# Inverting the delta-rule blocks of a prompt from 16-row pieces on 128 lanes instead of 32-row pieces on 64

## The chip, the cores and the metric

The kernel runs on one core of one Trainium2 chip. Its time is the device time of one execution in microseconds (us); a profiled execution gives besides it the span from the first to the last instruction, in which all traces below are read. TensorE is called PE in the profile, VectorE DVE, ScalarE ACT, GpSimdE POOL and SyncE SP; PEld is PE's loading of weights. Each has its own instruction queue and works through it in order.

## The reference, cut to what matters

The program is one decoder layer with two token mixers (sparse attention and gated DeltaNet) for a prompt of 256 tokens and a decode step of 8 sequences. The change lies in DeltaNet's prompt half, for 8 heads of width 128. In the reference's chunk step:

```python
L = jnp.exp(jnp.where(tril, dec[..., :, None] - dec[..., None, :], -jnp.inf))
kb = kc * bc[..., None]
A = jnp.where(stril, jnp.einsum('bhik,bhjk->bhij', kb, kc) * L, 0.0)
Tm = lax.linalg.triangular_solve(eye + A, jnp.broadcast_to(eye, A.shape),
                                 left_side=True, lower=True, unit_diagonal=True)
u = Tm @ vb
w = Tm @ (kb * jnp.exp(dec)[..., None])
```

What must be computed is the inverse of a unit lower-triangular matrix, for each head and chunk; `u` and `w`, the recurrence over chunks, the gate `z` and two projections follow from it. The kernel uses chunks of 128 tokens, so there are 2 chunks x 8 heads = 16 matrices of 128x128.

## The kernel before

**The stream of weights.** Nearly all of the work is a list `halves` of weight blocks of 128x1024 values. Each is loaded by SP (`raw`), split by ACT into a rounded part `hi` (L332) and by DVE into the rest `lo` (L333), and PE adds three products per 128x128 piece into the PSUM tile `acc`: a half is 24 matmuls with 264 columns (`three`, L316). `raw`, `hi` and `lo` have three buffers each, `acc` two. DVE also merges finished projections (`gate`, L1489; `zt`, L1468).

**Generators beside the stream.** Everything else (attention, decode, DeltaNet) is written as Python generators that are resumed by `tick()` twice per half; `yield n` lets n ticks pass. This order of writing, and then a scheduler with modelled durations, sets the order of the instructions on PE, DVE and ACT at build time. The order on SP and POOL is the order of writing. So a weight matmul may stand before, between or behind the matmuls of a generator, and on the chip each queue keeps the order that was fixed then.

**The inverse**, in `g_gdn`, L1187 to L1260. `At` (128 rows, 2 chunks, 8 heads, 128 columns) holds A. Diagonal blocks of 32 rows, 4 per matrix, 64 in all, are copied by four POOL DMAs to a DRAM tile `ad` (L1190), and from there into `lanes`, one block on each of 64 partitions (L1196). DVE inverts them row by row, i = 1 to 31, with one product of i*i values (L1203) and one sum over them (L1204) per row; both read and write 64 partitions. The result and its transpose go to the DRAM tile `td` (L1210, L1211) and back as diagonal blocks into `U` (L1215, 4 DMAs) and `TI` (L1218, 2 DMAs); `U` holds transposed inverses, `TI` plain ones. Two merge levels on PE double the blocks, 32 to 64 and 64 to 128. Each level goes over four quads (chunk t, four heads hg): a first matmul of A with U into a PSUM tile `inv`, a copy to SBUF by ACT (`P1`; at the last level also the transposed block, `T1`), a second matmul with the plain inverse, and a negated copy into U by DVE (L1239, L1259). `PG("inv")` takes turns in two PSUM banks. Then `uw` (L1270) multiplies U with the values and keys of each head, and `dS`, `og`, `vn` carry the recurrence.

**Slots.** Large tiles (`lanes`, `prod`, `U`, the decode states `sst`, ...) share 13 SBUF slots. A tile waits for the last reader of the one that had its slot. `TI` is the end of `prod`.

**Decode beside it.** `g_gdn_dec` runs at the same time: for each pair of sequences `sw` (16 matmuls), `swt` (4 transposes), `vnb` (16 transposes), with ACT and DVE updating the state `sst` (L1437, L1438), which is then written out as `o_Ss`.

## Time and profile before

| what | value |
|---|---|
| time, median of 3 runs | 1154.9 us (1154.56 to 1155.14) |
| profiled execution, its own time | 1156.45 us |
| its span | 1154.8 us |
| PE busy | 1116.2 us (97%) |
| DVE busy | 724.4 us (63%) |
| ACT busy | 570.6 us (49%) |
| POOL busy | 140.0 us (12%) |
| mean granted clock of PE | 0.981 |

The page says for each engine how long it was busy, then slices of the span, then the chain of work that ended last. A line of a group has the source line, engine, operation, `out<-in` by tile names, and shapes. A matmul of float32 data stands as two records in the trace, a weight matmul of the stream as one. In answers by windows, the numbers behind a stretch are its length, the busy time of PE, PEld, DVE, ACT and POOL with the number of instructions in brackets, the granted PE clock (1.00 is full), the DMA engines' share and GB/s.

### The profile page before, as it was taken

How to read it: one execution, taken by the hardware profiler on the slowest of the kernel's cores; microseconds unless marked ns; L12 is line 12 of the kernel's file. 1: busy time of each engine (PE TensorE's matmuls, PEld its weight loads, DVE VectorE, ACT ScalarE, POOL GpSimd, SP SyncE). 2: the span in 40 equal slices, each digit the busy share in tenths (PEclk: the TensorE clock that was granted, in tenths of full speed). 3: DMA queues.
4: the chain of work that ended last, by engine and by line, in shares of the span. 5: the costliest groups of instructions: out<-in, count | busy, mean ns of one | idle time of the engine just before them, and what ended most of it. 6: DMA issues, size and time to landing. Idle time of an engine off the chain costs nothing.

```text
span 1154.8 us, 24861 instructions
## 1 busy us (share of the span) xinstructions
PE 1116.2 (97%) x9334; PEld 1072.1 (93%) x9334; DVE 724.4 (63%) x1538; ACT 570.6 (49%) x1126; POOL 140.0 (12%) x217
## 2 busy tenths in 40 slices
PE   3999999999999999999999999999978999999998
PEld 3989999999999987897889999999967999999998
DVE  3487665444667766873565585679954565477543
ACT  4455655444634766773455465453421464444332
POOL 4420344100001320112113000000010000000000
PEclk9999999999999999999999999999985999999999
DMA  8874577335436874589979554664660345556663
GB/s 296 258 231 140 192 216 204 122 114 164 164 128 198 221 194 139 158 223 226 343 289 394 178 179 164 204 221 153 231 178 1 107 156 181 183 182 218 202 239 128
DMA packets 76843, 222.86 MB, mean 193 GB/s; under 512 B 10465, under 2 KB 27370, under 8 KB 75186
## 3 DMA queue, kind: packets, MB, share of 16 engines
q1 hardware_dynamic: 59346, 164.36, 43.3%
q0 software_dynamic: 14784, 45.70, 13.8%
q10 hardware_dynamic: 2592, 11.21, 2.6%
q8 instruction: 73, 1.20, 0.4%
q14 instruction: 48, 0.39, 0.1%
HBM read 203.23 MB, written 17.99 MB: 192 GB/s over the span
## 4 chain that ended last, share of the span: by engine, by line
PE 85%; DVE 6%; DMA 1%; issue 1%; ACT 0%; POOL 0%; POOLq 0%; ACTq 0%; DVEq 0%
PE acc L205 70%; DVE lanes L1204 2%; PE inv L205 1%; DVE lo L333 1%; PE po L205 1%; PE gtr L202 1%; PE pvo L205 1%; PE ps L205 1%; PE gsc L205 1%; PE cf L205 1%; DVE prod L1203 1%; PE kk L205 1%; PE vnb L202 1%; DMA U<-td 1%; DVE sst L1438 1%
## 5 line engine op out<-in xcount | busy, mean ns | idle before, releaser
L205 PE MATMUL acc<-xh,hi 128*128 128x264 f32 (+1 forms) x1488 | 433.5, 291 | 0.0
L332 ACT ACTIVATE hi<-raw 128x1024 fp32r<-128x1024 f32 (+1 forms) x250 | 264.0, 1057 | 334.6 <-PE acc L205 263.2
L205 PE MATMUL acc<-xh,lo 128*128 128x264 f32 (+1 forms) x1488 | 426.7, 287 | 2.2 <-DVE lo L333 2.2
L205 PE MATMUL acc<-xl,hi 128*128 128x264 f32 (+1 forms) x1488 | 427.4, 287 | 0.0
L333 DVE TENSOR_TENSOR lo<-raw,hi 128x1024 fp32r<-128x1024 f32 (+1 forms) x250 | 304.2, 1218 | 194.2 <-ACT hi L332 191.9
L205 PEld LDWEIGHTS acc<-xh,hi 128*128 128x128 f32 (+1 forms) x1488 | 281.3, 189 | 7.4 <-issue 7.0
L205 PEld LDWEIGHTS acc<-xh,lo 128*128 128x128 f32 (+1 forms) x1488 | 280.5, 188 | 4.6 <-DVE lo L333 2.6
L205 PEld LDWEIGHTS acc<-xl,hi 128*128 128x128 f32 (+1 forms) x1488 | 281.6, 189 | 1.4 <-issue 1.0
L205 PE MATMUL acc<-hi,w1h 128*128 128x254 f32 (+1 forms) x512 | 147.7, 289 | 16.5 <-ACT hi L409 16.5
L205 PE MATMUL acc<-lo,w1h 128*128 128x254 f32 (+1 forms) x512 | 146.4, 286 | 3.9 <-DVE lo L410 3.6
L205 PE MATMUL acc<-hi,w1l 128*128 128x254 f32 (+1 forms) x512 | 144.9, 283 | 0.0
L410 DVE TENSOR_TENSOR lo<-rawc,hi 128x512 fp32r<-128x512 f32 (+2 forms) x136 | 83.9, 657 | 51.4 <-ACT hi L409 46.2
L205 PEld LDWEIGHTS acc<-hi,w1h 128*128 128x128 f32 x512 | 97.8, 191 | 16.9 <-ACT hi L409 16.7
L409 ACT ACTIVATE hi<-rawc 128x512 fp32r<-128x512 f32 (+2 forms) x136 | 74.6, 599 | 58.8 <-PE acc L205 54.6
L205 PEld LDWEIGHTS acc<-lo,w1h 128*128 128x128 f32 x512 | 98.5, 192 | 5.2 <-DVE lo L410 5.0
L205 PEld LDWEIGHTS acc<-hi,w1l 128*128 128x128 f32 x512 | 98.2, 192 | 0.1
L386 POOL DMA_DIRECT2D rawc<-ccmp x125 | 67.6, 541 | 100.1 <-issue 71.2
L205 PE MATMUL acc<-oh,hi 128*128 128x264 f32 x256 | 73.3, 286 | 1.5 <-DVE gate L1489 1.4
L205 PE MATMUL acc<-mh,hi 128*128 128x264 f32 x256 | 72.6, 284 | 0.0
L205 PE MATMUL acc<-ol,hi 128*128 128x264 f32 x256 | 72.5, 283 | 0.0
L205 PE MATMUL acc<-ml,hi 128*128 128x264 f32 x256 | 72.5, 283 | 0.0
L205 PE MATMUL acc<-oh,lo 128*128 128x264 f32 x256 | 72.5, 283 | 0.0
(450 smaller groups left out, 1508.7 us busy)
## 6 DMA issues: line engine op xcount, KB each, us to landing
raw<-win SPq DMA_DIRECT2D x184, 512.0 KB, 3.5
raw<-wpab SPq DMA_DIRECT2D x32, 512.0 KB, 3.4
raw<-wo SPq DMA_DIRECT2D x32, 512.0 KB, 3.8
rawc<-ccmp SPq DMA_DIRECT2D x126, 128.0 KB, 3.1
rawc<-ccmp POOLq DMA_DIRECT2D x125, 128.0 KB, 3.2
raw<-w SPq DMA_DIRECT2D x8, 512.0 KB, 5.3
wk<-winK SPq DMA_DIRECT2D x8, 512.0 KB, 7.7
o_wk<-wk POOLq DMA_DIRECT2D x8, 512.0 KB, 8.6
```

The source lines that it names most:

```text
L202: T.transpose(out, in_, ident[0:n, 0:n])
L205: T.matmul(out, lhsT, rhs, start=start, stop=stop, **k)
L332: S.activation(self.hi, self.raw, AF.Copy)
L333: V.tensor_sub(self.lo, self.raw, self.hi)
L386: e.dma_start(rawc[kv, b][j // 8][:, j % 8].rearrange("p s c g -> p (s c g)"), src[kv, bass.ds(r, 1)].rearrange("o d f -> (o d) f"))
L409: S.activation(h, src, AF.Copy)
L410: V.tensor_sub(l, src, h)
L1203: V.tensor_tensor(pp, Lt[:, 0:i, 0:i], La[:, i, 0:i, None].to_broadcast([64, i, i]), ALU.mult)
L1204: V.tensor_reduce(Lt[:, i, 0:i], pp.rearrange("p j c -> p c j"), AX.X, ALU.add, negate=True)
L1438: V.scalar_tensor_tensor(ss[:, b, h, :], p4[:, 128 * hh:128 * hh + 128], k[:, c:c + 1], ss[:, b, h, :], ALU.mult, ALU.add)
```

## The change

Blocks of 16 rows instead of 32: 8 per matrix, 128 in all, one on each of the 128 partitions. Rows i = 1 to 15 instead of 1 to 31. `La` and `Lt` become part of `prod` (`lanes` is no longer a slot), `U` takes its slot before `prod` does, and U and TI are zeroed by DVE before the rows instead of U alone behind them. `ad` is filled by 8 DMAs instead of 4, U by 8 instead of 4, TI by 4 instead of 2. A merge level from 16 to 32 is added; at the level from 32 to 64 the plain inverse is made by multiplying U with the identity and copied to TI by ACT, since td no longer holds it. All three levels are written as `first`, `second`, `third` per quad, with the second matmul of one quad behind the first matmul of the next. The generator yields about as many ticks as before in all. Diff, with the last helper whole:

```diff
@@ -1184,80 +1184,102 @@
             yield 4
         del L["qkv", 1], kTg
 
-        ad = dp.tile([4, 16, 32, 32], F32, name="ad")
-        td = dp.tile([2, 4, 16, 32, 32], F32, name="td")
-        for k in range(4):
+        ad = dp.tile([8, 16, 16, 16], F32, name="ad")
+        td = dp.tile([2, 8, 16, 16, 16], F32, name="td")
+        for k in range(8):
             G.dma_start(ad[k].rearrange("h i j -> i h j"),
-                         At[32 * k:32 * k + 32, :, :, 32 * k:32 * k + 32].rearrange("i t h j -> i (t h) j"))
-        lanes = slot("lanes", [64, 2, 32, 32])
+                        At[16 * k:16 * k + 16, :, :, 16 * k:16 * k + 16].rearrange("i t h j -> i (t h) j"))
+        U = slot("U", [128, 2, 8, 128])
         prod = slot("prod", [128, 1536])
         TI = prod[:, 1024:1536].rearrange("p (h j) -> p h j", j=32)
+        lanes = prod[:, 256:768].rearrange("p (a i j) -> p a i j", a=2, i=16)
         La, Lt = lanes[:, 0], lanes[:, 1]
         G.dma_start(La.rearrange("p i j -> p (i j)"), ad.rearrange("k h i j -> (k h) (i j)"))
         V.memset(Lt, 0.0)
-        V.memset(lanes[:, 1].rearrange("p i j -> p (i j)")[:, ::33], 1.0)
+        V.memset(Lt.rearrange("p i j -> p (i j)")[:, ::17], 1.0)
+        V.memset(U, 0.0)
+        V.memset(TI, 0.0)
         yield 6
-        cost = 0
-        for i in range(1, 32):
-            pp = prod[0:64, 0:i * i].rearrange("p (j c) -> p j c", c=i)
-            V.tensor_tensor(pp, Lt[:, 0:i, 0:i], La[:, i, 0:i, None].to_broadcast([64, i, i]), ALU.mult)
+        for i in range(1, 16):
+            pp = prod[:, 0:i * i].rearrange("p (j c) -> p j c", c=i)
+            V.tensor_tensor(pp, Lt[:, 0:i, 0:i], La[:, i, 0:i, None].to_broadcast([128, i, i]), ALU.mult)
             V.tensor_reduce(Lt[:, i, 0:i], pp.rearrange("p j c -> p c j"), AX.X, ALU.add, negate=True)
-            cost += 0.4 + 2 * i * i / 960.0
-            if cost > 2.2:
-                cost = 0
-                yield 2
+            if i % 3 == 2:
+                yield
         V.tensor_copy(La, Lt.rearrange("p i j -> p j i"))
         G.dma_start(td[0].rearrange("k h i j -> (k h) (i j)"), Lt.rearrange("p i j -> p (i j)"))
         G.dma_start(td[1].rearrange("k h i j -> (k h) (i j)"), La.rearrange("p i j -> p (i j)"))
-        U = slot("U", [128, 2, 8, 128])
-        V.memset(U, 0.0)
-        for k in range(4):
-            G.dma_start(U[32 * k:32 * k + 32, :, :, 32 * k:32 * k + 32].rearrange("i t h j -> i (t h) j"),
-                         td[1, k].rearrange("h i j -> i h j"))
+        for k in range(8):
+            G.dma_start(U[16 * k:16 * k + 16, :, :, 16 * k:16 * k + 16].rearrange("i t h j -> i (t h) j"),
+                        td[1, k].rearrange("h i j -> i h j"))
             if k % 2 == 0:
-                G.dma_start(TI[32 * k:32 * k + 32], td[0, k].rearrange("h i j -> i h j"))
-        yield 5
-        for t in range(2):
-            for hg in range(2):
-                p1 = PG("inv")
+                G.dma_start(TI[16 * k:16 * k + 16, :, 0:16], td[0, k].rearrange("h i j -> i h j"))
+        yield 8
+        quads = [(t, hg) for t in range(2) for hg in range(2)]
+
+
+        def first(w, t, hg):
+            p1 = PG("inv")
+            for hh in range(4):
+                h = 4 * hg + hh
+                if w < 64:
+                    rhs = U[:, t, h, :].rearrange("p (c k j) -> p c k j", k=2, j=w)[:, :, 1, :]
+                    mm(p1[:, 64 * hh:64 * hh + 64].rearrange("p (c j) -> p c j", j=w), At[:, t, h, :], rhs)
+                else:
+                    mm(p1[0:64, 64 * hh:64 * hh + 64], At[64:128, t, h, 0:64], U[64:128, t, h, 64:128])
+            if w == 64:
                 for hh in range(4):
-                    h = 4 * hg + hh
-                    rhs = U[:, t, h, :].rearrange("p (c k j) -> p c k j", c=2, k=2)[:, :, 1, :]
-                    mm(p1[:, 64 * hh:64 * hh + 64].rearrange("p (c j) -> p c j", c=2), At[:, t, h, :], rhs)
-                yield 5
-                P1 = tp.tile([128, 256], F32, name="P1", tag="a", bufs=NA)
-                S.activation(P1, p1[:, 0:256], AF.Copy)
-                yield
-                p2 = PG("inv")
+                    tr(p1[0:64, 256 + 64 * hh:320 + 64 * hh], U[0:64, t, 4 * hg + hh, 0:64])
+            elif w == 32:
                 for hh in range(4):
                     for c in range(2):
                         pr = slice(64 * c, 64 * c + 32)
-                        o = 64 * hh + 32 * c
-                        mm(p2[pr, o:o + 32], TI[pr, 8 * t + 4 * hg + hh, :], P1[pr, o:o + 32])
-                p2v = p2[:, 0:256].rearrange("p (h c j) -> p h c j", h=4, c=2)
+                        mm(p1[pr, 256 + 32 * hh:288 + 32 * hh], U[pr, t, 4 * hg + hh, 64 * c:64 * c + 32],
+                           ident[pr, 64 * c:64 * c + 32])
+            return p1
+
+        def second(w, t, hg, p1):
+            n = 64 if w == 64 else 128
+            P1 = tp.tile([128, 256], F32, name="P1", tag="a", bufs=NA)
+            S.activation(P1[0:n], p1[0:n, 0:256], AF.Copy)
+            if w == 64:
+                T1 = tp.tile([128, 256], F32, name="T1", tag="a", bufs=NA)
+                S.activation(T1[0:64], p1[0:64, 256:512], AF.Copy)
+                inv = lambda pr, h: T1[0:64, 64 * (h % 4):64 * (h % 4) + 64]
+            elif w == 32:
                 for c in range(2):
-                    V.tensor_scalar(U[64 * c:64 * c + 32, t, 4 * hg:4 * hg + 4, 64 * c + 32:64 * c + 64],
-                                    p2v[64 * c:64 * c + 32, :, c, :], -1.0, None, ALU.mult)
-        for t in range(2):
-            for hg in range(2):
-                p1 = PG("inv")
-                for hh in range(4):
-                    h = 4 * hg + hh
-                    mm(p1[0:64, 256 + 64 * hh:320 + 64 * hh], At[64:128, t, h, 0:64], U[64:128, t, h, 64:128])
-                for hh in range(4):
-                    tr(p1[0:64, 64 * hh:64 * hh + 64], U[0:64, t, 4 * hg + hh, 0:64])
-                yield 2
-                P1 = tp.tile([128, 256], F32, name="P1", tag="a", bufs=NA)
-                T1 = tp.tile([128, 256], F32, name="T1", tag="a", bufs=NA)
-                S.activation(P1[0:64], p1[0:64, 256:512], AF.Copy)
-                S.activation(T1[0:64], p1[0:64, 0:256], AF.Copy)
-                yield 2
-                p2 = PG("inv")
-                for hh in range(4):
-                    o = slice(64 * hh, 64 * hh + 64)
-                    mm(p2[0:64, o], T1[0:64, o], P1[0:64, o])
-                V.tensor_scalar(U[0:64, t, 4 * hg:4 * hg + 4, 64:128], p2[0:64, 0:256].rearrange("p (h j) -> p h j", h=4),
-                                -1.0, None, ALU.mult)
+                    pr = slice(64 * c, 64 * c + 32)
+                    S.activation(TI[pr, 8 * t + 4 * hg:8 * t + 4 * hg + 4, :],
+                                 p1[pr, 256:384].rearrange("p (h j) -> p h j", h=4), AF.Copy)
+            if w < 64:
+                inv = lambda pr, h: TI[pr, 8 * t + h, :]
+            return P1, inv
+
+        def third(w, t, hg, P1, inv):
+            p2 = PG("inv")
+            nc_ = 64 // w
+            for hh in range(4):
+                for c in range(nc_):
+                    pr = slice(2 * w * c, 2 * w * c + max(w, 32))
+                    o = 64 * hh + w * c
+                    mm(p2[pr, o:o + w], inv(pr, 4 * hg + hh), P1[pr, o:o + w])
+            for c in range(nc_):
+                pr = slice(2 * w * c, 2 * w * c + w)
+                V.tensor_scalar(U[pr, t, 4 * hg:4 * hg + 4, 2 * w * c + w:2 * w * c + 2 * w],
+                                p2[pr, 0:256].rearrange("p (h c j) -> p h c j", h=4, c=nc_)[:, :, c, :], -1.0, None, ALU.mult)
+
+        for w in (16, 32, 64):
+            held = None
+            for q in range(5):
+                if q < 4:
+                    p1 = first(w, *quads[q])
+                    yield 3
+                if held:
+                    third(w, *held)
+                    yield 1 if q < 4 else 2
+                held = (*quads[q], *second(w, *quads[q], p1)) if q < 4 else None
+                if q == 3:
+                    yield 2
         uu = vbt
         wT = slot("wT", [128, 8, 256])
         for h in range(8):
```

The change moves instructions. Three places follow.

**PE, at the inverse.** Behind the decode matmuls `sw` of the third pair of sequences the program before has 600 weight matmuls of the stream and then the whole inverse in one piece (`acc` is the stream, `inv<-U,At` a first matmul, `inv<-P,prod` a second one):

```order
L205 MATMUL acc<-xh,lo 128x264
L205 MATMUL inv<-U,At 128x64 x4
L205 MATMUL inv<-P_12266,prod 32x32 x8
L205 MATMUL inv<-U,At 128x64 x4
L205 MATMUL inv<-P_12393,prod 32x32 x8
```

In the changed program 233 weight matmuls stand there, `sw` of the fourth pair moves behind the first matmul, and the stream goes on between the pieces:

```order
L205 MATMUL acc<-xl,hi 128x264
L205 MATMUL inv<-U,At 128x64 x8
L205 MATMUL acc<-xh,lo 128x264
...
L205 MATMUL inv<-P_11909,prod 32x16 x16
L205 MATMUL inv<-U,At 128x64 x4
L202 MATMUL swt<-cst,swr 128x128 x4
L205 MATMUL acc<-xh,hi 128x264
...
L205 MATMUL inv<-P_12013,prod 32x16 x16
L205 MATMUL inv<-U,At 128x64 x4
L202 MATMUL vnb<-cst,dvn 128x128 x8
```

The first lines left out are 15 weight matmuls, the second 19. From the first `inv` to the last `uw` matmul the new order has 393 weight matmuls between them, where before there were 19, all at the end. In it PE goes 16 times from the stream to matmuls on 32 or 64 partitions of the array (the second matmuls, the identity products, the whole last level) and back; before, four such pieces of second matmuls and the last level lay side by side without the stream.

**POOL, the copies through DRAM.** The whole of POOL's difference, without line numbers that only shift:

```order
-L1190 DMA ad<-At 32x16x32 x4
-L1196 DMA lanes<-ad 64x1024
-L1215 DMA U<-td 32x16x32
-L1218 DMA prod<-td 32x16x32
-L1215 DMA U<-td 32x16x32 x2
+L1190 DMA ad<-At 16x16x16 x8
+L1197 DMA prod<-ad 128x256
+L1213 DMA U<-td 16x16x16
+L1216 DMA prod<-td 16x16x16
+L1213 DMA U<-td 16x16x16 x2
```

The pieces of U and TI (shown as `prod`) are 12 issues instead of 6, each half as many elements per run and half as many runs. The ninth to twelfth wait for the landing of the first, second, third and fourth, because POOL's DMAs use eight semaphores in turn.

**DVE, the beginning of the rows.** `lo` is the split of a weight block. Before, with five splits between the clearing of the lanes and row 1:

```order
L1197 MEMSET lanes 64x1024
L333 TENSOR_TENSOR lo<-raw,hi 128x1024
L1471 TENSOR_TENSOR ol<-zt,oh 128x264
L1198 MEMSET lanes 64x32
L333 TENSOR_TENSOR lo<-raw,hi 128x1024 x2
L1438 SCALAR_TENSOR_TENSOR sst<-vnb,dcv,sst 128x128 x4
L333 TENSOR_TENSOR lo<-raw,hi 128x1024
L1489 SCALAR_TENSOR_TENSOR gate<-gate,acc 128x264
L333 TENSOR_TENSOR lo<-raw,hi 128x1024
L1203 TENSOR_TENSOR prod<-lanes 64x1
```

In the changed program:

```order
L1198 MEMSET prod 128x256
L1201 MEMSET prod 128x512
L1199 MEMSET prod 128x16
L333 TENSOR_TENSOR lo<-raw,hi 128x1024
L1493 TENSOR_TENSOR ol<-zt,oh 128x264
L1205 TENSOR_TENSOR prod<-prod 128x1
L1206 TENSOR_REDUCE prod<-prod 128x1
L1205 TENSOR_TENSOR prod<-prod 128x4
L1206 TENSOR_REDUCE prod<-prod 128x2
L333 TENSOR_TENSOR lo<-raw,hi 128x1024
```

Row 1 now stands behind the first of those splits, the others between the rows; the clearing of U (2048 values) stands between the product and the sum of row 11 and waits for the write `o_Ss` of the state that had its slot.

## The prediction

> **What bounds the kernel now.** First the page: PE is busy nearly throughout, the chain that ended last runs mostly through the weight stream, and the clock row is full but for two dips.
>
> ```profile
> span 1154.8 us, 24861 instructions
> PE 1116.2 (97%) x9334; PEld 1072.1 (93%) x9334; DVE 724.4 (63%) x1538; ACT 570.6 (49%) x1126; POOL 140.0 (12%) x217
> PEclk9999999999999999999999999999985999999999
> PE acc L205 70%; DVE lanes L1204 2%; PE inv L205 1%; DVE lo L333 1%; PE po L205 1%; PE gtr L202 1%; PE pvo L205 1%; PE ps L205 1%; PE gsc L205 1%; PE cf L205 1%; DVE prod L1203 1%; PE kk L205 1%; PE vnb L202 1%; DMA U<-td 1%; DVE sst L1438 1%
> ```
>
> So time is lost only where PE waits, runs slowly, or has work added. Both of the chain's rare engines (DVE `lanes`, DMA `U<-td`) and the deep dip belong to the inverse. Next the waits of PE between 620 and 955 us, the place of the dip: all that is over 1 us is the inverse or follows from it.
>
> ```profile
> PE inv L205 <- DMA U<-td: 5.4, 1, 5.4
> PE acc L205 <- DVE lo L333: 2.2, 1, 2.2
> PE inv L205 <- ACT P L1229: 1.9, 4, 0.5
> PE uw L205 <- ACT wT L1276: 1.8, 3, 1.1
> PE inv L205 <- ACT T L1253: 1.6, 2, 0.8
> PE acc L205 <- DVE gate L1489: 1.4, 1, 1.4
> ```
>
> These are 14.3 us. The windows show that the clock takes more. Stretches cut where PE's work changes; the last row counts stream matmuls alone.
>
> ```profile
> 774.98:844.04 69.06, 65.35 (x562) 64.44 (x559) 67.72 (x102) 31.86 (x55) 0.53 (x1) 1.00 0.54 182
> 844.04:857.21 13.17, 13.17 (x94) 12.96 (x94) 8.94 (x8) 3.27 (x4) 4.47 (x7) 0.87 0.76 233
> 857.21:862.58 5.37, 0.00 (x0) 0.00 (x0) 1.23 (x1) 0.97 (x1) 0.00 (x0) 0.92 1.04 202
> 862.58:899.27 36.69, 31.39 (x246) 27.79 (x247) 17.82 (x75) 7.39 (x22) 0.00 (x0) 0.59 0.11 42
> 947.42:1154.80 207.38, 204.22 (x1690) 204.00 (x1689) 114.55 (x147) 83.38 (x102) 0.00 (x0) 1.00 0.56 189
> ...
> 774.98:844.04 69.06, 63.31 (x507) 61.73 (x507) 4.99 (x12) 1.48 (x4) 1.00 0.54 182
> ```
>
> The last stretch prices a stream matmul: 204.22/1690 = 0.1208 us. In the first DVE is busy 67.72 of 69.06 us with rows and splits; from 862.58 to 899.27 there is no stream on PE and the mean clock is 0.59. Prices of the other work, from the chain in order of time:
>
> ```profile
> 767.71 0.56 PE sw L205 x10
> 774.26 0.79 PE sw L205 x22
> 781.05 0.44 PE swt L202 x4
> 862.58 1.98 PE inv L205 x8
> 865.02 2.55 PE inv L205 x24
> 877.08 1.60 PE inv L205 x16
> 878.68 0.57 PE inv L202 x4
> 921.13 1.78 PE og L205 x16
> ```
>
> A record of a 128-column float32 matmul is 1.78/16 = 0.111 us at full clock, a transpose 0.44/4 = 0.11. The `inv` rows ran at clock 0.50 and are halved below.
>
> **What the change removes.** Losses are the stretch less its work at full clock.
> - 774.98 to 844.04: 507 x 0.1208 = 61.2, twenty transposes 2.2, a `sw` group 1.0 (below); 64.4. Lost: 4.6.
> - 844.04 to 857.21: 94 x 0.1208 = 11.4. Lost: 1.8, to the low clock behind the 2.2 us wait.
> - 857.21 to 862.58: the wait for U, 5.4.
> - 862.58 to 899.27: four quads of 24 records, 4 x 2.55/2 = 5.1; four of the last level, 4 x (1.60 + 0.57)/2 = 4.3; the other 70 records (`swt`, `vnb`, `uw`) x 0.11 = 7.7; 17.1. Lost: 19.6.
>
> Together 31.4 us. I take all of it as removable: DVE's 31 rows shrink to 15 of at most 225 values, and 393 stream matmuls (47.5 us) stand between the first `inv` and the last `uw`, which hides hand-offs to ACT, DVE and DMA. If that cover were gone, the 5.4 + 1.9 + 1.8 + 1.6 us of waits would be back, and the clock with them.
>
> **What it adds on PE.**
> - Level 16: 16 first matmuls, 32 records of 1.98/2/8 = 0.124: 4.0 us.
> - 64 second matmuls and 32 identity products, 192 records. At half clock 16 such took 2.55 - 1.98 = 0.57, 0.036 each; bounds 0.018 (scales) and 0.036. From the two `sw` rows the slope is (0.79 - 0.56)/12 = 0.019 at full clock, so 3.6 us (3.4 to 6.9).
> - Going to pieces of the array and back. The same two rows leave 0.56 - 10 x 0.019 = 0.37 us for a group of any size inside the stream; a 16-matmul `sw` group is so 0.37 + 0.61 = 1.0. Between float32 matmuls at half clock the 0.57 left no such constant. Bounds 0 and 0.37; the nearest row has the stream on both sides, as here: 16 x 0.37 = 5.9 us (0 to 5.9).
>
> Added: 13.5 us (7.4 to 16.8). The Trainium skill, "TensorEngine Tiling (Array Packing)", section Key Properties, says that a change of tiling mode, not merely of tile, drains the array. It speaks against cutting the inverse into the stream; the constant 0.37 in the `sw` rows agrees. Without it the time would come out 5.9 us lower.
>
> **What it moves: is U ready in time?** PE reaches the first `inv` 233 stream matmuls behind 774.98: 28.1 us, at 803.1. U's path:
>
> ```profile
> L1196 POOL DMA_DIRECT2D lanes<-ad x1: 555/555/555, 756.2 to 756.2; - x1
> lanes<-ad POOLq DMA_DIRECT2D x1, 256.0 KB, 5.1
> 770.36 0.15 DVE L1203 TENSOR_TENSOR prod<-lanes 64x1 f32<-64x1 f32 x1 [0.36 <-DMA o_Ss<-sst]
> 786.76 0.54 DVE L1204 TENSOR_REDUCE lanes<-prod 64x15 f32<-64x225 f32 x1
> 845.12 1.01 DVE lanes L1209
> 846.41 5.43 DMA td<-lanes
> 856.10 6.44 DMA U<-td
> L1215 POOL DMA_DIRECT2D U<-td x4: 652/656/684, 852.8 to 856.1; - x4
> L1213 DVE MEMSET U<- 128x2048 f32 x1 | 1.8, 1765 | 0.4 <-issue 0.4
> ```
>
> Row 1 waited until 770.36 for the state write in `prod`'s slot; now that wait goes to U's clearing, and row 1 starts when the lanes have landed: 756.2 + 5.1 = 761.3. Rows 1 to 15, with their splits between, took 786.76 + 0.54 - 770.36 = 16.9 us; U's clearing 1.8; two more splits and one decode update that now fall between, and the copy, some 4 (an estimate from the order and the rows' pace): 784. From the copy's end at 846.13 to 862.58 were 16.4 us; six more issues of 0.66 add 3.9; so U is complete at 804. I take 1 us of waiting (0, if half as much data lands sooner, to 3, if the semaphore waits of the last issues cost more than their turn). Behind DVE's wait at row 1 a split is queued about 2 us, which PE needs only two halves (5.8 us) later.
>
> Costed at nothing: four more `ad` issues (2.6 us of POOL, hidden in its 30 us wait for the lanes' slot), the clearing of TI, and the TI copies (ACT had 7.39 busy of 36.69 us in the inverse); uncovered they would be 2.6, 0.5 and about 2 us. For the new hand-offs in the stream I take 2 us (0 to 6): the rows of waits show `uw` losing 1.8 where PE had no stream to cover.
>
> **Sum.** 31.4 - 13.5 - 1 - 2 = 14.9 us less. The profiled span becomes 1139.9, its own time 1156.45 - 14.9 = 1141.6; the median of the runs stands 1.55 under the profiled execution, so 1154.9 - 14.9 = **1140.0 us**. With all bounds good 31.4 - 7.4 = 24 (1131), all bad 31.4 - 16.8 - 9 = 5.6 (1149).
>
> **Rivals.**
> *U late, clock low.* If the last four issues, each behind an earlier landing, wait a full flight of 6.4 us, PE waits 7 us at 803. The clock then falls: two-microsecond windows behind the 2.2 us wait and in the inverse read
>
> ```profile
> 842.00:844.00 2.00, 0.00 (x0) 0.00 (x0) 2.00 (x3) 0.57 (x1) 0.53 (x1) 1.00 0.00 0
> 846.00:848.00 2.00, 2.00 (x11) 2.00 (x11) 1.62 (x2) 0.00 (x0) 0.55 (x1) 0.50 0.95 340
> 880.00:882.00 2.00, 1.97 (x20) 1.80 (x20) 0.42 (x1) 0.52 (x2) 0.00 (x0) 0.50 0.00 0
> 632.00:634.00 2.00, 2.00 (x16) 2.00 (x16) 0.00 (x0) 0.00 (x0) 0.00 (x0) 0.76 1.01 419
> 450.00:460.00 10.00, 10.00 (x57) 7.15 (x57) 3.57 (x9) 3.16 (x5) 1.95 (x2) 1.00 0.42 117
> ```
>
> and with half the work around it in small matmuls some 9 us would run at half speed: 6 + 4.5 more, 1150.5. Against: six DMAs in flight at once landed within 6.4 us of the last issue. The Trainium skill, "TensorE: Matmul & The Clock Gate", section Why this matters for your kernels, warns of idle gaps over about 3 us; here 2.2 us was enough, so by its rule a wait of 3 us would be free and by this trace it is not.
>
> *Hand-offs stay serial.* Two `inv` banks serve all quads. If each of 24 hand-offs (three levels, four quads, two each) stops PE for the 0.5 us that `P` cost before, 12 us go: 1150, and with the low clock that follows sparse PE work, 1155, no difference. For: the second matmul needs the bank that ACT empties. Against: at nearly every hand-off the order has 7 to 24 stream matmuls, 0.8 to 2.9 us.
>
> *Slower: the clock falls in the mixture and stays.* At 632 PE was fully busy and the clock fell, so small matmuls do not hold it. If the mixture from the first to the last `inv` (295 stream matmuls, 35.6 us, and about 26 of the rest) ran at 0.50, it would take 62 us more: 1202. It is slower than before from 14.9 us at half speed on. Against: attention mixes small matmuls and stream at 1.00 (window 450 to 460), and here no run without stream is longer than about 3 us.
>
> **Chances.** Forecast 0.74; U late 0.16; serial 0.05; clock 0.05. The forecast's own band is 1133 to 1147; the range 1130 to 1150 holds it, the good bound, and about half of the late case. Two executions are told apart from about 0.2%, 2.3 us, so faster means under 1152.6: the forecast and nearly all of the late case, 0.89; same 0.05 (serial); slower 0.06 (clock, and the tail of the late case).
>
> **What would show it.** Right: PEclk at 1.00 from 800 to 900 us, no PE wait for `U<-td` over 3 us, the first `inv` near 804, no DVE-caused wait at 820 to 844, and PE's `inv` groups inside the stream. The sum of `inv` records at level 16 shows the 4.0 and 3.6, the gap around each small group the 0.37. Wrong: a clock of 0.5 behind the first `inv`, or waits of PE on ACT and DVE that add up to more than 10 us between 800 and 880.

## The result and the profile after

The changed kernel takes 1138.48 us (median of 4 runs, 1134.57 to 1139.12), the kernel before 1155.02 us beside it (1154.56 to 1156.85): a ratio of 0.9847, 95% interval 0.9822 to 0.9872. A later set of five runs gave 1136.70 against 1156.87 us, ratio 0.9825 (0.9806 to 0.9844). The forecast was 1140.0 us.

The page of the profiled execution, whose own time is 1137.88 us: PE's share, the clock row, and the chain of work that ended last.

```profile
span 1136.2 us, 25323 instructions
PE 1112.4 (98%) x9558; PEld 1069.3 (94%) x9558; DVE 697.1 (61%) x1523; ACT 572.7 (50%) x1138; POOL 144.2 (13%) x227
PEclk9989999999999999999999899999999999999999
PE 92%; DVE 1%; ACT 0%; issue 0%; ACTq 0%
PE acc L205 77%; PE inv L205 1%; PE po L205 1%; PE gtr L202 1%; PE pvo L205 1%; PE ps L205 1%; PE gsc L205 1%; PE cf L205 1%; PE kk L205 1%; PE vnb L202 1%; PE uw L205 1%; DVE xt L306 1%; PE pst L202 0%; PE og L205 0%; PE wsc L205 0%; PE kvtr L202 0%
```

The rows of the blocks and the DMA of U are gone from the chain, and so is the deep dip at the end of the clock row. Asked for PE's waits from 620 to 955 us, the trace answers with no row at all, where before there were six of over 1 us. The windows, columns as in the prediction; the first three are the stretches up to the first `inv`, from the first to the last one, and `uw`, the fourth is the stream alone at the end, and the fifth the whole stage, from the `sw` matmuls of the third pair of sequences (their second part) to the last `ogt` transposes behind the recurrence:

```profile
776.26:804.51 28.25, 28.25 (x236) 28.25 (x234) 17.09 (x24) 13.19 (x22) 7.80 (x14) 1.00 0.68 200
804.51:867.72 63.21, 63.21 (x781) 59.66 (x780) 34.80 (x89) 27.49 (x61) 0.00 (x0) 1.00 0.44 144
867.72:885.28 17.56, 17.56 (x155) 17.56 (x153) 15.90 (x55) 6.87 (x12) 0.00 (x0) 1.00 0.52 180
929.53:1136.20 206.67, 203.25 (x1682) 203.04 (x1681) 114.60 (x146) 83.31 (x102) 0.00 (x0) 1.00 0.58 190
775.47:928.93 153.46, 153.46 (x1555) 149.72 (x1555) 93.59 (x215) 73.11 (x166) 8.37 (x15) 1.00 0.48 155
```

And the whole stage of the kernel before, between the same two events:

```profile
774.19:946.82 172.63, 158.25 (x1323) 153.32 (x1323) 124.76 (x243) 70.81 (x154) 5.58 (x9) 0.90 0.43 140
```

PE is busy for all of the 153.46 us, at full clock. The stage is 172.63 - 153.46 = 19.2 us shorter and holds 886 stream matmuls instead of 878 (counted in the order of the instructions), so that 8 x 0.1208 = 1.0 us of work came into it besides: **20.1 us are gained there**. The medians moved by 16.5 in one set and 20.2 in the other, the spans of the two profiled executions by 18.6. In these two executions the other 1.5 us lie where nothing was changed. Windows of the changed kernel and then of the one before, at two places far ahead of the inverse, each with the one long wait of PE near 72 us:

```profile
72.00:82.00 10.00, 9.41 (x52) 9.15 (x53) 7.11 (x16) 1.16 (x3) 3.93 (x8) 0.66 0.88 277
632.00:642.00 10.00, 10.00 (x62) 10.00 (x62) 3.12 (x8) 3.21 (x7) 0.00 (x0) 0.66 1.00 365
...
72.59 0.58 PE L205 MATMUL acc<-lo,w1h 128*128 128x254 f32 x1 [2.56 <-DVE lo L410]
```

```profile
72.00:82.00 10.00, 7.39 (x60) 7.11 (x59) 9.62 (x19) 3.23 (x8) 3.24 (x6) 1.00 0.80 258
632.00:642.00 10.00, 10.00 (x59) 10.00 (x60) 1.90 (x7) 1.49 (x3) 0.00 (x0) 0.66 0.91 329
...
74.78 0.39 PE L205 MATMUL acc<-lo,w1h 128*128 128x254 f32 x1 [2.60 <-DVE lo L410]
```

The wait is the same in both (the last section says what makes the difference). Behind it the changed kernel's execution did 6.2 us of work at half clock, 3.1 us lost, and the other none; near 29 us the other lost 1.7 us in the same way (half clock from 28.88 to 32.29). In the executions profiled below, the window at 72 us stood between 0.66 and 1.00 and the one at 632 us between 0.66 and 0.83. So kernels are compared below by the length of the stage, less 0.1208 us for each stream matmul in it, beside the medians:

| kernel | stage, us | stream matmuls in it | rest, us | median, us | ratio to before (95%) |
|---|---|---|---|---|---|
| before | 172.63 | 878 | 66.6 | 1155.02 | |
| changed | 153.46 | 886 | 46.4 | 1138.48 | 0.9847 (0.9822 to 0.9872) |
| changed, second set | 153.46 | 886 | 46.4 | 1136.70 | 0.9825 (0.9806 to 0.9844) |
| 32 rows, pipelined merges | 169.11 | 875 | 63.4 | 1152.19 | 0.9964 (0.9951 to 0.9977) |
| 16 rows, merges one by one | 152.80 | 886 | 45.8 | 1135.50 | 0.9821 (0.9803 to 0.9838) |
| slots the other way round | 153.46 | 886 | 46.4 | 1137.24 | 0.9847 (0.9816 to 0.9878) |
| U ten us later | 153.55 | 878 | 47.5 | 1137.49 | 0.9856 (0.9834 to 0.9878) |
| merges gathered | 139.60 | 782 | 45.1 | 1133.88 | 0.9801 (0.9781 to 0.9820) |

### The profile page after: what moved, and what is told of

It is laid out like the page before. It is cut to its first block, busy times and chain, and to the rows that moved or that the text cites. A ratio compares the mean times of both kernels' runs of the same rounds, so it can differ in the third digit from the quotient of the medians.

```text
span 1136.2 us, 25323 instructions
## 1 busy us (share of the span) xinstructions
PE 1112.4 (98%) x9558; PEld 1069.3 (94%) x9558; DVE 697.1 (61%) x1523; ACT 572.7 (50%) x1138; POOL 144.2 (13%) x227
## 4 chain that ended last, share of the span: by engine, by line
PE 92%; DVE 1%; ACT 0%; issue 0%; ACTq 0%
PE acc L205 77%; PE inv L205 1%; PE po L205 1%; PE gtr L202 1%; PE pvo L205 1%; PE ps L205 1%; PE gsc L205 1%; PE cf L205 1%; PE kk L205 1%; PE vnb L202 1%; PE uw L205 1%; DVE xt L306 1%; PE pst L202 0%; PE og L205 0%; PE wsc L205 0%; PE kvtr L202 0%
```

## The experiments

Two theories stood against each other. Theory 1: the gain comes from U being complete while stream work is left that covers the merges. Theory 2: it comes from interleaving the quads.

**One part alone: the pipelined merges.** Blocks, lanes, rows and DMAs as before, the merges written with `first`, `second`, `third`:

```diff
-        for t in range(2):
-            for hg in range(2):
-                p1 = PG("inv")
...
+        for w in (32, 64):
+            held = None
+            for q in range(5):
+                if q < 4:
+                    p1 = first(w, *quads[q])
+                    yield 3
+                if held:
+                    third(w, *held)
...
```

> Blocks of 32 rows on 64 lanes, the 31 rows, the DMAs and the slots stay as in the kernel before; only its two merge levels are written as after the change (second matmul of one quad behind the first of the next, same yields per level). Theory 1 (the gain comes from U being complete while stream work is left): the order still has 5568 stream matmuls ahead of the first inv matmul, as before, so U still comes at about 862, PE waits some 5 us, the clock falls, and no stream is left beside the merges; only hand-off waits shrink (1.9 + 1.6 us before): 1150 to 1155 us. Theory 2 (the gain comes from interleaving the quads): near the changed kernel or below it, since one level less is to be computed, 1132 to 1143 us.

Measured 1152.19 us: theory 1. PE's waits from 620 to 960 us, and one stretch of windows:

```profile
PE inv L205 <- DMA U<-td: 5.9, 1, 5.9
PE acc L205 <- DVE lo L333: 2.2, 1, 2.2
PE acc L205 <- DVE gate L1502: 1.5, 2, 1.4
PE uw L205 <- ACT wT L1289: 1.4, 2, 0.9
PE inv L205 <- PE inv L205: 0.2, 1, 0.2
...
862.00:887.00 25.00, 24.58 (x196) 21.91 (x197) 8.10 (x35) 5.52 (x16) 0.00 (x0) 0.50 0.05 21
```

The hand-off waits on `P` and `T` are gone, as interleaving should do it, which gave 3.2 us. But the clock stood at 0.50 for 25 us in which PE was busy 24.58. So the loss in the dry merges was not waiting at hand-offs: it was the clock, with PE at work.

**The other part undone: merges one by one.**

```diff
         for w in (16, 32, 64):
-            held = None
-            for q in range(5):
...
+            for q in range(4):
+                p1 = first(w, *quads[q])
+                yield 3
+                P1, inv = second(w, *quads[q], p1)
+                yield
+                third(w, *quads[q], P1, inv)
+            yield 3
```

> The changed kernel with its three merge levels unpipelined: each quad's first matmul, copy and second matmul one after the other, with about the same number of ticks in all (60 for 57). The order puts 5201 stream matmuls ahead of the first inv matmul, as in the changed kernel. Theory 1 (U early, stream as cover): within 3 us of the changed kernel's 1138.5, since 7 to 27 stream matmuls still stand at each hand-off. Theory 2 (interleaving): the hand-off waits come back at twelve quads, 0.5 us at each of 24 hand-offs, and the clock with them: 1148 us or more.

Measured 1135.50 us, no wait of PE between 620 and 960 us, clock 1.00 from 660 on; the rest of the stage is 0.6 us shorter than with pipelining. Theory 2 falls from both sides: with the stream around them, the merges need no interleaving.

**The order of the slots.**

```diff
-        U = slot("U", [128, 2, 8, 128])
         prod = slot("prod", [128, 1536])
+        U = slot("U", [128, 2, 8, 128])
```

> The changed kernel, but prod (which holds the lanes) takes its slot before U does, so that the lanes and the rows wait for the state write again, which was over at about 772 us in the changed kernel's trace. PE's order is the same as in the changed kernel, 5201 stream matmuls ahead of the first inv. Row 1 then starts at about 775 instead of 760.6 and U is complete at about 813 instead of 799: PE, which comes to the first inv at 804.5, waits some 8 us. If the clock falls behind this wait (the rival of the prediction: about 9 us of work at half speed, 4.5 us lost): 1138.5 + 8 + 4.5 = 1151 us. If the clock holds: 1146.5 us. If the order of slots does not matter: 1138.5 us.

The stage is the same to 0.01 us, since U did not come later; so the run says nothing about a late U. DVE's timeline (start, duration, idle time before it in brackets):

```profile
758.39 0.16 DVE L1205 TENSOR_TENSOR prod<-prod 128x1 f32<-128x1 f32 x1 [1.58 <-DMA prod<-ad]
769.96 1.76 DVE L1200 MEMSET U<- 128x2048 f32 x1 [1.03 <-DMA o_Ss<-sst]
```

Row 1 ran without the state write, and the clearing of U waited for it, which no one needs before 790. That is so in the changed kernel too: DVE's instructions stand in the same order with the same waits in both, so the order of these two lines does not decide which tile waits, and this run is a second execution of the changed kernel. What it confirms is a step of the prediction: the wait has gone from the rows to U's clearing.

**U ten us later.** Sixteen DMAs that nobody reads, in front of those that fill U:

```diff
+        for k in range(16):
+            G.dma_start(tx[k // 8, k % 8], td[1, k % 8])
         for k in range(8):
             G.dma_start(U[16 * k:16 * k + 16, :, :, 16 * k:16 * k + 16].rearrange("i t h j -> i (t h) j"),
```

> The changed kernel with sixteen more DMAs on POOL's queue ahead of those that fill U (copies of td that nobody reads, so work is added and none left out), some 0.56 us of issuing each: U comes about 9 us later, at about 808. The order, made at build time, allows for it: 5329 instead of 5201 stream matmuls ahead of the first inv (at about 820), and 263 up to the last uw instead of 393. If U only has to come while enough stream work is left (theory 1), this costs nothing: within 2 us of the changed kernel, no wait of PE beside the merges. If each us by which U is late is paid: 9 us more, 1146.

The last DMA into U was issued at 803.91 instead of 794.02 us, and PE came to the first `inv` at 819.36 instead of 804.51, so it did not wait for U. Measured 1137.49 us; the rest of the stage is 1.1 us longer, 0.8 of it one wait of `uw` for ACT. Ten us of delay cost one: U only has to come while enough stream work is left. What a U costs for which PE has to wait in the changed kernel was not measured.

**Why the stream ran dry: the tile zt.** In the order of the kernel before, no stream matmul stands between the first and the last `inv`. The finished z projections wait in the two `acc` banks for their merge tile `zt` (L1466), which takes turns in the ring of five buffers with P1, T1 and kbe of the inverse, written earlier. First only `zt` was taken out of the ring, into one buffer:

```diff
-            t = tp.tile([128, TT], F32, name="zt", tag="a", bufs=NA)
+            t = tp.tile([128, TT], F32, name="zt", tag="zt", bufs=1)
```

> The kernel before, with 32-row blocks, but the merge tile zt of the finished z projections gets one buffer of its own instead of a turn in the ring of five that the inverse and kbe use (and jk, used elsewhere, goes into that ring for room). The order then has 5616 stream matmuls ahead of the first inv instead of 5568. If the stream ran dry because finished projections could not be merged, 48 more stream matmuls (5.8 us) fill the wait for U of 5.4 us: 1149.5 us with the clock still at 0.5 in the merges behind it; if the fall of the clock came from that wait alone, the merges run at full clock too and some 10 to 15 us are gained: 1140 to 1145 us. If the ring was not the cause: 1155 us.

1172.30 us, slower than before (1.0139, 1.0113 to 1.0164), which neither theory expected. The first `zt` was written at 859.46 instead of 895.93, so the ring did hold it up. But its merge needs the recurrence's result, at 930.09, and holds the only buffer until then; the second z projection kept its bank, and no stream matmul ran from the first `inv` at 870 to 932:

```profile
863.00:932.00 69.00, 54.49 (x434) 48.83 (x432) 35.49 (x117) 23.88 (x79) 0.66 (x2) 0.76 0.21 64
...
859.46 0.37 ACT L1467 ACTIVATE zt<-acc 128x264 f32<-128x264 f32 x1
...
930.09 0.43 DVE L1469 SCALAR_TENSOR_TENSOR zt<-zt,oB 128x264 f32<-128x264 f32 x1 [1.71 <-ACT oB L1337]
```

So the other tiles were taken out instead, and the five buffers left to the stream:

```diff
-                P1 = tp.tile([128, 256], F32, name="P1", tag="a", bufs=NA)
+                P1 = prod[:, 512 * t + 256 * hg:512 * t + 256 * hg + 256]
...
-            kb = tp.tile([128, 2, 128], F32, name="kbe", tag="a", bufs=NA)
+            kb = prod[:, 256 * (h % 4):256 * (h % 4) + 256].rearrange("p (t d) -> p t d", t=2)
```

> The kernel before, with its 32-row blocks, 31 rows and unpipelined merges, but the tiles P1, T1 and kbe of the inverse and of uw lie in prod and lanes, which nobody reads any more by then, instead of in the ring of five buffers that the merge tile zt of the stream uses too. The order then has 5582 stream matmuls ahead of the first inv (5568 before), 196 between the first and the last inv (none before), and 85 more up to the last uw (19 before). Theory 1a (the dry stream of 36.7 us in the kernel before came from that ring, not from the late U as such): the 19.6 us lost there come back, the wait for U is 5.4 - 1.7 = 3.7 us with a few us of low clock behind it: 1136 to 1143 us, as good as the changed kernel although U is as late as before. Theory 1b (a late U by itself leaves nothing to cover the merges): the stream matmuls that now stand beside the merges are missing later, and the time stays at 1150 to 1155 us. The larger move of zt alone (one buffer, slower by 16 us) speaks for neither: there the second z projection had to wait for the end of the recurrence.

1147.92 us (0.9929, 0.9909 to 0.9948): about half of the gain, between the two expectations. The merges and `uw`, with a U as late as before (PE waited 2.6 us for it, until 860.27), and then the recurrence:

```profile
PE ogt L202 <- DVE oG L1327: 7.0, 2, 6.6
PE inv L205 <- DMA U<-td: 2.6, 1, 2.6
...
860.00:900.00 40.00, 39.73 (x407) 37.74 (x408) 22.70 (x59) 15.03 (x26) 0.00 (x0) 1.00 0.40 137
936.00:952.00 16.00, 8.04 (x35) 6.84 (x36) 10.34 (x31) 7.37 (x23) 0.58 (x1) 0.57 0.18 66
```

From 860 to 900 nothing is lost, at full clock, though it is the old inverse. But the stream may run ahead of the recurrence's end only as far as five buffers and two banks hold z projections; the matmuls that stood beside the merges were missing at the end of it, where PE then stood and the clock fell. Both halves of theory 1 count: the place of the stream, and how early U is.

**What keeps the clock down.** First the waits alone, in the last 200 us, where PE has only the stream: `hi` is written up to nine times more.

```diff
-            S.activation(self.hi, self.raw, AF.Copy)
+            for _ in range(1 + getattr(self, "slow", 0)):
+                S.activation(self.hi, self.raw, AF.Copy)
```

> The changed kernel, but five of the last 32 halves (the first halves of output blocks 2, 5, 8, 11 and 14, where PE has nothing but stream matmuls) get their rounded part hi written 4, 5, 6, 7 and 9 times more, 1.06 us each, so that PE waits for them some 0.7, 1.8, 2.8, 3.9 and 6.0 us (estimated from hi 1.06 and lo 1.2 us and two halves of 2.9 us of lead). Read is the granted clock behind each wait. If a wait of 2.2 us is enough by its length, as the prediction read from the kernel before: 1.00 behind the first two, 0.5 for some 4 us behind the other three, time 1138 + 15 + 3 x 2.2 = 1160 us. If the limit lies higher and something else helped there: 1.00 behind the waits of 2.8 and perhaps 3.9 us too, 1153 to 1158 us.

1165.32 us; the waits were longer than estimated. The first of the five halves gave two waits of 0.45; the others 2.29, 3.38, 4.47 and 6.69 us. Windows around the first two, at the wait of 2.29, behind it, and behind that of 3.38:

```profile
1049.00:1055.00 6.00, 5.12 (x40) 4.68 (x39) 3.89 (x4) 2.53 (x3) 0.00 (x0) 1.00 0.33 98
1069.00:1072.00 3.00, 0.71 (x6) 0.55 (x4) 1.03 (x2) 2.37 (x3) 0.00 (x0) 1.00 0.00 0
1072.00:1076.00 4.00, 3.50 (x17) 3.32 (x16) 2.90 (x3) 0.00 (x0) 0.00 (x0) 0.58 0.54 187
1096.00:1100.00 4.00, 3.98 (x20) 3.98 (x21) 2.24 (x2) 0.00 (x0) 0.00 (x0) 0.57 0.66 214
```

Behind the four waits from 2.29 us on, 3.4, 3.4, 4.6 and 5.3 us of stream ran at half clock, so 1.7 to 2.6 us were lost each time. Then float32 matmuls of 128x64, like the `first` of a merge, were added between the stream matmuls: 60 of them without a wait, the same wait of 3.4 us alone, and 13 and 47 behind another such wait.

```diff
+                    if part == 0 and n != 6:
+                        p = PG("dum")
+                        for j in range(60):
+                            o = 64 * (j % 8)
+                            mm(p[:, o:o + 64], ident, half.hi[:, j % 8, 0:64].bitcast(F32))
```

> The changed kernel with work added in the last sixteen output blocks, where PE otherwise has only stream matmuls, to see what kept the clock at 0.5 in the dry merges (in the kernel with pipelined 32-row merges PE was busy 24.58 of 25 us from 862 to 887 and the clock still 0.50). First, 60 float32 matmuls of 128x64 (120 records, 14 us at full clock) in the middle of a half, with no wait ahead. Then a wait of some 3.4 us alone (hi written 6 times more), and later the same wait with the 60 float32 matmuls right behind it. Nobody reads their results. Theory A (such work without stream holds the clock down once it has fallen): 1.00 in the first block, about 4.3 us at 0.5 behind the lone wait, and 0.5 through nearly all of the third block, some 28 us. Theory B (the clock comes back by itself about 4 us after any wait): 0.5 for some 4.3 us in the third block too, then 1.00. Theory C (such work lowers the clock by itself): below 1.00 in the first block already.

The rows are the 60 without a wait, the stretch behind the lone wait, the 13 with ten stream matmuls behind the wait, and the last 47:

```profile
1052.00:1065.00 13.00, 13.00 (x119) 13.00 (x118) 0.86 (x1) 0.00 (x0) 0.00 (x0) 1.00 0.18 64
1090.00:1094.00 4.00, 3.27 (x13) 2.96 (x14) 3.35 (x3) 0.62 (x1) 0.00 (x0) 0.59 0.24 61
1118.00:1128.00 10.00, 8.63 (x40) 8.63 (x41) 3.50 (x3) 1.28 (x2) 0.00 (x0) 0.50 0.45 157
1128.00:1138.00 10.00, 10.00 (x91) 10.00 (x90) 0.00 (x0) 0.00 (x0) 0.00 (x0) 0.98 0.01 2
```

Theory C is out: the first 60 ran at full clock. Between A and B this run does not decide, because ten stream matmuls came between the 13 and the 47. Then 120 in one piece right behind the wait (the same lines, called ahead of the half's own matmuls):

> As the run before, but now 120 float32 matmuls of 128x64 (240 records, 27 us at full clock, 54 at half) in one piece right behind the second wait of 3.4 us, ahead of the half's stream matmuls; the first wait stands alone again. In the run before, the lone wait was followed by some 4 us at 0.5, the one with 13 such matmuls behind it by 9.7 us, and the clock was back after ten stream matmuls; the 47 matmuls behind these ran at 1.00. Theory A (plain float32 work holds the clock down until stream matmuls run): 0.5 through the whole block, some 50 us. Theory B (the clock comes back by itself after some 10 us at most): 0.5 for up to 10 us, then 1.00 within the block.

Half clock through the whole block, as theory A has it. Three windows inside the block, and one behind it:

```profile
1110.00:1125.00 15.00, 15.00 (x72) 15.00 (x72) 0.00 (x0) 0.00 (x0) 0.00 (x0) 0.50 0.22 77
1125.00:1140.00 15.00, 15.00 (x72) 15.00 (x72) 0.00 (x0) 0.00 (x0) 0.00 (x0) 0.50 0.00 1
1140.00:1155.00 15.00, 15.00 (x72) 15.00 (x72) 0.00 (x0) 0.00 (x0) 0.00 (x0) 0.50 0.00 1
1170.00:1180.00 10.00, 10.00 (x85) 10.00 (x85) 4.83 (x6) 3.62 (x4) 0.00 (x0) 1.00 0.67 221
```

PE was busy without a gap for the 51 us of the block, all at half clock; after 4 us of stream it was back. The same matmuls at full clock leave it there. So they neither lower the clock nor bring it back. In the kernel before, the wait of 5.4 us for U lowered the clock, and the merges behind it, without stream, could not raise it. The data type alone is not the reason, for there the clock came back without stream, at 892.45 us, while PE ran float32 `uw` matmuls and transposes of 128 columns:

```profile
890.08 1.91 PE L202 MATMUL vnb<-cst,dvn 128*128 128x128 f32 x8
891.78 0.63 PE L205 MATMUL uw<-vbt,U 128*128 128x128 f32 x2
...
892.78 0.39 PE L205 MATMUL uw<-U,kbe 128*128 128x128 f32 x2
```

The number of columns alone was not varied.

**The price of a group of small pieces.** Groups on constants in the same stretch:

```diff
+        kind = {3: (1, 32, 16), 4: (1, 32, 16), 5: (16, 32, 16), 6: (16, 32, 16), 7: (64, 32, 16), 8: (64, 32, 16),
+                9: (16, 32, 32), 10: (16, 32, 32), 11: (1, 128, 128), 12: (1, 128, 128), 13: (8, 128, 64)}.get(n)
+        if kind:
+            at_end(dummy)
```

> The changed kernel, with extra float32 matmuls on constants that nobody reads (so work is added, none left out) at the ends of both halves of eleven of the last sixteen output blocks, where PE has nothing but stream matmuls: groups of 1, 16 and 64 pieces of 32x16, 16 pieces of 32x32, 1 full 128x128 and 8 full 128x64 matmuls, two groups or four of each. Read is what each adds to the 24 stream matmuls around it. The prediction's terms: a group of small pieces 0.37 us + 0.019 per record (two records a piece): 0.41, 0.98 and 2.8 us; a full 128x128 0.22 us and nothing besides. If going to pieces costs nothing by itself: 0.04, 0.61, 2.4. From the changed kernel's own trace, in which 32 records took 0.37 and 64 took 0.66 us: 0.009 per record and about 0.2 to 0.4 for the group, so 0.3, 0.6 and 1.4.

Read from the start of the last whole stream matmul ahead of a group to that of the second one behind it, less two intervals of 0.12 us:

```profile
1072.90 0.28 PE L205 MATMUL acc<-mh,lo 128*128 128x264 f32 x1
1073.12 0.44 PE L205 MATMUL dum<-cst 32*32 32x16 f32 x32
1073.48 0.39 PE L205 MATMUL acc<-mh,hi 128*128 128x264 f32 x1
1073.71 0.28 PE L205 MATMUL acc<-ml,hi 128*128 128x264 f32 x1
```

0.81 - 0.24 = 0.57 us for 32 records (16 pieces). In the same way 0.43 for 4 records, 1.40 for 128, and 0.23 for one full 128x128 (two records). From 32 records on that is 0.30 + 0.0086 a record; the smallest group costs 0.43. Full-sized float32 matmuls cost nothing besides their records. The Trainium skill, "TensorEngine Tiling (Array Packing)", section Key Properties, says that a change of tiling mode drains the array; by that only the groups of pieces pay an entrance, and these rows agree, with 0.30 to 0.43 us.

**A faster version: the merges gathered.** All four quads of a level at a time, in 7 groups of pieces instead of 16:

```diff
+        for w in (16, 32):
...
+            for t in range(2):
+                p = PG("inv")
+                for h in range(8):
+                    for c in range(c_):
+                        pr = slice(2 * w * c, 2 * w * c + 32)
+                        o = 64 * h + w * c
+                        mm(p[pr, o:o + w], TI[pr, 8 * t + h, :], prod[pr, 512 * t + o:512 * t + o + w])
```

> The changed kernel's blocks, rows and DMAs; the three merge levels take all four quads at a time (levels 16 and 32: 16 first matmuls, two copies of 512 columns, all 64 or 32 second matmuls, at level 32 all 32 identity products in one group; level 64: two quads' first matmuls, twice, then all 16 second ones). The same matmuls, in 7 groups of small pieces instead of 16, and the first inv 27 stream matmuls earlier. If a group costs 0.37 us besides its records, as the prediction took from the sw rows: 9 x 0.37 = 3.3 us below the changed kernel's 1138.5, 1135. If it costs 0.2: 1.8 us, 1136.7. If grouping costs nothing: 1138.5. If fewer quads beside each other leave PE waiting at the hand-offs (7 instead of 24): up to 3 us above the changed kernel.

1133.88 us (1131.77 to 1135.77, five runs) beside the changed kernel's 1136.70 (1135.43 to 1138.83).

> The changed kernel again, beside the gathered one on the same chip: 1138.5 us, within 3 us.

The rest of the stage is 1.3 us shorter, with one new wait of 0.5 us in it. If that is all due to the groups, nine groups less save 1.8 us, 0.2 each, below the 0.30 between stream matmuls on both sides; in the changed kernel half of the 16 groups have a full-sized float32 matmul next to them. The other 1.5 us between the medians lie outside the stage: the window at 632 us stood at 0.83 in the profiled execution of the gathered kernel and at 0.66 in that of the changed one beside it.

## Why the prediction was right, step by step

- **Losses, 31.4 us, all removable: right.** The stage has no wait and no slow stretch left. The share of 19.6 us had the right size and place, and its remedy, stream matmuls as cover, is what the old inverse with the ring freed showed (1.00 from 860 to 900). What the step did not say is why 14.3 of the 19.6 us were lost with PE at work (31.39 us busy for 17.1 us of work): the merges cannot raise a clock that has fallen.
- **Added work, 13.5 us: too much.** The stage gives 31.4 - 20.1 = 11.3 us for it. The term of 0.019 a small record was over twice the measured 0.0086, outside its own bounds (192 x 0.0086 = 1.7 us instead of 3.6): the slope between two `sw` rows does not hold for pieces of 32x32. The 0.37 for going to pieces was right. With 0.112 us for each of the 32 records of the first matmuls (3.6 us; measured on constants in the stream) and 1.7 us for the small ones, 6.0 of the 11.3 us are left for 16 groups, 0.38 each; on constants a group cost 0.30 to 0.43 inside the stream, and the nine groups that gathering takes away 0.2.
- **U in time, at 804 with 1 us of wait: the wait did not come, U was some 4 us earlier.** The copy was done at 782.8 instead of 784; an issue took 0.56 us instead of 0.66:

```profile
783.07 0.54 POOL L1211 DMA_DIRECT2D td<-prod  x1 [0.55 <-DVE prod L1209]
787.20 0.59 POOL L1213 DMA_DIRECT2D U<-td  x1 [3.58 <-DMA td<-prod]
792.91 0.56 POOL L1213 DMA_DIRECT2D U<-td  x1 [0.68 <-DMA prod<-td]
794.02 0.56 POOL L1213 DMA_DIRECT2D U<-td  x1
...
U<-td POOLq DMA_DIRECT2D x8, 16.0 KB, 5.7
```

  With 5.7 us from issue to landing U was complete near 800, before PE came at 804.51.
- **Hand-offs, 2 us: none.** No wait of PE on ACT or DVE is left, and even merges one by one cost none.
- **The sum.** 14.9 us forecast, 20.1 in the stage: 3 us of waits that did not come and 2.2 of added work. That the median stood only 1.5 us under the forecast is partly luck: in the profiled executions the changed kernel lost 3.1 us behind the wait near 72 us, which cost the other nothing, and the other 1.7 us near 29 us.
- **The rivals.** U late: its condition did not arise, and the order, made with the DMAs' durations in view, shifts the first `inv` when U is later (128 stream matmuls for ten us). Its price of 4.5 us for the low clock depends on what follows the wait: with stream alone 1.7 to 2.6 us were lost, with 13 float32 matmuls of 128x64 behind the wait 4.5 (8.9 us of work at half clock). A wait of 2.2 us can lower the clock, as it took, but its length alone does not decide (last section). Serial hand-offs: refuted by the merges one by one. The clock falling in the mixture: 1.00 throughout.

## What to carry to other kernels

Where one engine's steady stream covers everything else, look at the stage in which it runs dry, and ask what holds the stream: here a merge tile in a ring that it shared with the work it should have covered. A shorter side chain pays until it ends while cover is left; ten us of delay within that cost one, and taking the interleaving away again cost nothing. Taking one buffer out of a shared ring may cost more than it frees when the tile waits for the end of the same chain. And a difference of a few us between two profiled executions may lie far from the change, so compare the stage.

## What the runs showed of the hardware

- In all 14 traces the granted clock changes on a grid of 3.41 us: every stretch at half clock lasts 3.41 us or a multiple of it (6.83, 10.24, 30.72 and 54.61 among them), but for the last one, which the end of the program cuts off. Where PE had only stream in a step of this grid, half clock followed whenever PE stood for 1.77 us or more of the step, and never when it stood for 1.72 us or less. So the place of a wait counts besides its length. The wait of 2.20 us in the kernel before lay in one step, and the clock fell; that of 2.57 us in the kernel with the ring freed lay in two, 1.60 and 0.98, and the clock held. Near 72 us PE waits 2.56 to 2.60 us in every trace; behind it the clock fell in eight and held in six.
- The Trainium skill, "TensorE: Matmul & The Clock Gate", section Why this matters for your kernels, allows idle gaps up to about 3 us; the runs go against that at 2.2 and 2.29 us.
- The Trainium skill, "TensorE: Matmul & The Clock Gate", section Why this matters for your kernels, asks for some 4 us of continuous work to reach the full clock. 51 us of continuous float32 matmuls of 128x64 did not reach it here; with stream matmuls it took about 4 us. What counts as work for the clock is not what the profile counts as busy.
- Around 632 us the clock falls in every trace with PE busy throughout, for 3.41 us in two and 6.83 us in twelve. PE has hardly any stream there, but for about 5 us float32 records of 8 columns, 40 in all (`smo`, `dec`). In the changed kernel:

```profile
632.47 2.30 PE L205 MATMUL smo<-cst,X 128*128 128x8 f32 x20
...
634.62 1.36 PE L205 MATMUL dec<-smt,cst 128*128 128x8 f32 x8
```

  So float32 records of 8 columns went with a falling clock, those of 64 columns neither lowered nor raised it, and `uw` with 128 columns, among transposes, went with a rising one. That the number of columns decides is a guess from these three.
- Falls of the clock make most of the spread of these runs: the changed kernel's run of 1134.57 us had a mean clock of 0.998, that of 1139.12 us 0.994, and 0.4% of the span is 4.5 of the 4.6 us between them.
